# Seven products of quarters for the first MLP product of a two-layer trunk

## The chip, the cores and the metric

The kernel runs as one program on one core of a Trainium2 chip. The metric is the device time of one execution in microseconds. The kernel before takes 1731.39 us, the median of three runs (1730.09, 1731.39, 1732.92).

## The reference, cut to what matters

A trunk of two layers works on 16 learned and 512 given tokens of 1024 features, all in float32. Each layer is a sequence mixer and an MLP, each followed by a LayerNorm of the scaled input plus the result. The change touches the MLP alone:

```python
D_MODEL = 1024; D_FF = 4 * D_MODEL; DEPTH = 2

def sq_relu_mlp(h, w1, w2):
    return jnp.square(jax.nn.relu(h @ w1)) @ w2

# in each of the two layers, after the mixer:
h = layer_norm(DN_ALPHA * h + mix, ln1_w[i], ln1_b[i])
h = layer_norm(DN_ALPHA * h + sq_relu_mlp(h, mlp_w1[i], mlp_w2[i]), ln2_w[i], ln2_b[i])
```

Layer 0 has 528 tokens in its MLP. In layer 1 the 16 learned tokens are no longer needed there, so it has 512.

## The kernel before, in words

Everything is kept feature-major: 128 features on the partitions, tokens along the row. A float32 operand is kept as a pair, a rounded high part and the rest as a low part. One product of a 128 x 128 weight tile with a row of tokens is then three matmuls: high by high (line L173), high weight by low row (L174), low weight by high row (L175). A weight tile of 128 outputs by 1024 inputs is loaded by SyncE's queue (SP, L157, buffers `wr`, of which there are two) and split 512 columns at a time: ScalarE (ACT) rounds it into `wh` (L152), VectorE (DVE) subtracts into `wl` (L153). There are six buffers of each.

The 4096 hidden features of an MLP are taken in four groups of eight tiles. For each group, `mlp` first makes the eight tiles of `h @ w1`, eight steps of 128 inputs each. Each tile's sum in PSUM goes through ReLU (ACT, L381), a square in full precision (GpSimd, POOL, L383), a rounded square (ACT, L389) and the low part of it (DVE, L390). Then the eight output tiles take the product of this group with w2, again eight steps each, and DVE adds each sum from PSUM to a residual kept in SBUF (L363; in the first group L367 and L368, from the input of the MLP).

In layer 0 the 528 tokens are two halves of 272 and 256 columns. In layer 1 the two halves of 256 fit in one matmul of 512 columns; only the first three w1 tiles and the last three w2 tiles keep the halves apart, so that the norm before can still be under way and the norm after can begin with one half.

The order of the instructions on each engine is fixed when the program is built. The code is written as generators that are interleaved, and a scheduler then gives each engine its list. Each engine takes its list in order and waits at an instruction whose inputs or buffers are not ready. PSUM has eight banks, three for these sums (`pmm`) and five others (`pmx`).

Of the kernel before, what the change touches and what calls it, by code (L numbers as in the profile page):

```python
# [18 lines left out]
P = 128  # L19
# [38 lines left out]
def trunk(ctx: ExitStack, tc: tile.TileContext, a, out):  # L58
# [11 lines left out]
    NBUF = {"s": 40, "m": 20, "n": 40, "row": 3}  # L70
# [56 lines left out]
    # ---------------------------------------------------------------- constants  # L127
# [22 lines left out]
    # ---------------------------------------------------------------- weights  # L150
# [26 lines left out]
    def product(o, blks, xs, m=P, k0=0, k1=None, every=8):  # L177
        """o[m, n] += sum over k0 <= k < k1 of blks[k]^T xs[k]"""
        per = 512 // P if m == P else 8
        n = len(xs)  # L180
        for k in range(k0, k1 or n):
            hi, lo = blks[k // per]
            c = (k % per) * m
            mm3(o, (hi[:, c:c + m], lo[:, c:c + m]), xs[k], k == 0, k == n - 1)
            if k % every == every - 1 and k < n - 1:
                tick()

    def phase(tiles, rhs, evac, ns, head=0, tail=0, ready=None):
        """tiles: list of (srcs, key[, m]); rhs[half][k] = (hi, lo) APs, rhs[2] both halves where they fit a
        bank. In the first and the last tiles the halves are apart, so that what precedes and follows can  # L190
        work on one half at a time."""
        def both(blks, key):
            o = pm(512)
            product(o, blks, rhs[2], every=4)
            for hf in range(2):
                evac(key, hf, o[:, hf * 256:hf * 256 + 256])
            tick()

        def run(hf, blks, key, m=P):
            o = pm(ns[hf], part=m)  # L200
            product(o, blks, rhs[hf], m=m)
            evac(key, hf, o)
            tick()
        n = len(tiles)
        for i0, i1 in [(0, head)] + [(i, i + 1) for i in range(head, n - tail)] + [(n - tail, n)]:
            held = []
            for srcs, *key in tiles[i0:i1]:
                held.append(([b for s in srcs for b in (s if isinstance(s, list) else wload(s))], *key))
# [50 lines left out]
    def layernorm(r, ns, hf, go, apply, together=False):  # L259
        """statistics of the tokens of a half as its sums r come, then apply(off, bn, pt, mean, rstd, i)"""  # L260
# [49 lines left out]
    def norm_after(r, ns, wcol, bcol):  # L310
        """tasks for both halves, each from when its sums have been emitted"""
# [35 lines left out]
    def residual(hx, offs, ns, early=()):  # L347
        """evac into r = alpha * h + product"""
# [24 lines left out]
    def mlp(l, hx, ns, ready, r, evac0):  # L373
        w1, w2 = a["mw1"], a["mw2"]
        for c in range(4):
            u = [[None] * 8 for _ in hx]

            def evac_u(f, hf, o):
                n = ns[hf]
                t = tl("m", n)  # L380
                S.activation(t, o, AF.Relu)  # L381
                q = tl("m", n)
                G.tensor_tensor(q, t, t, op=MUL)  # L383
                if hf == 0:
                    pair = tl("s", L, F32R), tl("s", L, F32R)
                    for dst, x in zip(u, parts(pair, ((0, n), (n, ns[1]), (0, 512)))):
                        dst[f] = x
                hi, lo = u[hf][f]
                S.activation(hi, t, AF.Square)  # L389
                V.tensor_tensor(lo, q, hi.bitcast(F32), op=SUB)  # L390

            phase([([w1[l, c * 8 + f]], f) for f in range(8)], hx, evac_u, ns,
                  head=3 if c == 0 else 0, ready=ready if c == 0 else None)
            phase([([w2[l, c, m]], m) for m in range(KT)], u,
                  lambda m, hf, o: evac0(m, hf, o, last=c == 3), ns, tail=3 if c == 3 else 0)

    # ---------------------------------------------------------------- shared pieces
# [15 lines left out]
    def conv_job(src, wc, bcol, done):  # L413
        """projection through conv and silu, feature-major [128, L]"""
# [30 lines left out]
    def gate_job(src, width, task):  # L445
        """small projection, then a task on its sums"""
# [10 lines left out]
    def gate_task(fm, width):  # L457
        """token-major [128, 5, width] with unused rows zero"""
# [9 lines left out]
    def decay(dt_in, bias, alog, nh):  # L468
        """g = -exp(A_log) softplus(x + bias), sums over chunks and their exponentials"""
# [17 lines left out]
    # ================================================================ layer 0 mixer  # L487
# [15 lines left out]
    # scratch in DRAM for the diagonal blocks of 32: a pitch of 129 rows makes the 68 blocks equidistant  # L503
# [26 lines left out]
    def gdn_keys(hd):  # L530
# [3 lines left out]
        # decays between the tokens of a chunk  # L534
# [16 lines left out]
        # similarities of the keys; the squared norms are on their diagonal  # L551
# [32 lines left out]
    def gdn_base():  # L584
        """diagonal blocks of 32, one to a partition: forward substitution"""
# [341 lines left out]
    hn, _, ready = norm_after(r, ns0, PP_LN, PP_LN + 8)  # L927
# [4 lines left out]
    mlp(0, h, ns0, ready, r, ev)  # L932
    h = hn

    # ================================================================ layer 1 mixer
# [27 lines left out]
    def hb(ap):  # L963
        """[128, heads] over the 64 features of a head"""
# [188 lines left out]
    hn, _, ready = norm_after(r, ns1, PP_LN + 32, PP_LN + 40)  # L1153
    # the first products begin with the groups that are ready
# [20 lines left out]
    def finish(hf):  # L1175
# [16 lines left out]
        def last(blocks):  # L1192
            """both blocks at once, over the engines; what needs the mean alone comes first"""
# [23 lines left out]
    mlp(1, h, ns1, ready, r, ev)  # L1217
# [101 lines left out]
```

## Time and profile before

| | |
|---|---|
| median of the runs | 1731.39 us |
| span of the profiled execution, which is also its time from the first instruction to the last | 1727.4 us |
| TensorE (PE) busy | 1690.1 us, 98% |
| DVE, ACT, POOL busy | 1015.5, 680.0, 324.1 us |
| mean granted TensorE clock | 0.995 |
| DMA | 157.99 MB, 91 GB/s |

An engine's idle time costs nothing unless TensorE waits for it. A row of a group of instructions has the source line, the engine, the operation, the names of the tile written and of those read, their shapes, the count, then the busy time in us and the mean of one in ns, and last the idle time before them and what ended it. PEld is TensorE's loading of weights, which runs beside its matmuls.

### The profile page before, as it was taken

Reading aid. Unit: us, or ns where it says so; the run is one execution under the profiler, and the core shown is the slowest. Engines: PE = TensorE matmul, PEld = TensorE weight load, DVE = VectorE, ACT = ScalarE, POOL = GpSimd, SP = SyncE. Lnnn points to the kernel's source line nnn. Section 1 sums busy time; section 2 is a strip of 40 time slices with the busy share of each in tenths; the row PEclk is TensorE's granted clock in tenths of the full one; section 3 lists DMA queues with packets and bytes.
Section 4 is the critical chain, followed back from the end, with each engine's and each line's share of the span. In section 5 each row is a group of like instructions: output and inputs, shape, how many; then the busy total and the mean of one; then the engine's idle time right before and its main releaser. Section 6 shows DMA issues by size and latency. Waiting matters only on the chain.

```text
span 1727.4 us, 29456 instructions
## 1 busy us (share of the span) xinstructions
PE 1690.1 (98%) x11644; PEld 1537.0 (89%) x11644; DVE 1015.5 (59%) x2116; ACT 680.0 (39%) x1455; POOL 324.1 (19%) x380
## 2 busy tenths in 40 slices
PE   9999999999999999999999999999999999999997
PEld 8899998899999999999999878888788888888886
DVE  6896667676436443343348767868753744444345
ACT  4432345554225333242425634554432533333331
POOL 1311211010004111010202245242400411101012
PEclk9999999999999999999999999999999999999999
DMA  7224211112222222222221443333222222222221
GB/s 252 69 86 121 77 63 62 38 63 85 98 66 82 92 92 87 98 87 89 96 72 61 131 133 88 99 110 111 80 79 98 73 86 98 98 98 89 94 98 61
DMA packets 80325, 157.99 MB, mean 91 GB/s; under 512 B 12668, under 2 KB 45820, under 8 KB 79932
## 3 DMA queue, kind: packets, MB, share of 16 engines
q1 hardware_dynamic: 80044, 155.86, 28.2%
q8 instruction: 91, 1.49, 0.4%
q14 instruction: 46, 0.38, 0.1%
q10 hardware_dynamic: 144, 0.26, 0.0%
HBM read 149.95 MB, written 6.15 MB: 90 GB/s over the span
## 4 chain that ended last, share of the span: by engine, by line
PE 84%; DVE 6%; DMA 3%; POOL 3%; ACT 2%; issue 2%; SPq 0%; POOLq 0%; DVEq 0%; ACTq 0%
PE pmm L173 24%; PE pmm L175 24%; PE pmm L174 24%; DMA row<-rd 2%; DVE s L407 2%; DVE wl L153 2%; POOL row L985 1%; PE pmx L271 1%; POOL hl L341 1%; DMA wr<-in_w 1%; PE pmx L331 1%; PE pmx L1049 1%; PE pmx L1045 1%; POOL n L147 1%; PE pmx L753 1%
## 5 line engine op out<-in xcount | busy, mean ns | idle before, releaser
L173 PE MATMUL pmm<-hh,wh 128*128 128x272 f32 (+4 forms) x2104 | 652.3, 311 | 2.3 <-ACT wh L152 0.9
L174 PE MATMUL pmm<-hl,wh 128*128 128x272 f32 (+4 forms) x2104 | 638.5, 304 | 2.7 <-POOL hl L341 2.1
L175 PE MATMUL pmm<-hh,wl 128*128 128x272 f32 (+4 forms) x2104 | 640.3, 304 | 0.1
L153 DVE TENSOR_TENSOR wl<-wr,wh 128x512 fp32r<-128x512 f32 (+1 forms) x498 | 376.2, 759 | 319.8 <-ACT wh L152 313.5
L152 ACT CAST wh<-wr 128x512 fp32r<-128x512 f32 (+1 forms) x498 | 306.6, 619 | 628.3 <-PE pmm L174 605.1
L173 PEld LDWEIGHTS pmm<-hh,wh 128*128 128x128 f32 (+2 forms) x2104 | 393.5, 187 | 25.0 <-issue 4.4
L174 PEld LDWEIGHTS pmm<-hl,wh 128*128 128x128 f32 (+2 forms) x2104 | 393.6, 187 | 24.4 <-POOL hl L341 4.6
L175 PEld LDWEIGHTS pmm<-hh,wl 128*128 128x128 f32 (+2 forms) x2104 | 393.5, 187 | 17.0 <-DVE wl L153 0.3
L173 PE MATMUL pmm<-s,wh 128*128 128x256 f32 (+2 forms) x1192 | 377.9, 317 | 0.0
L175 PE MATMUL pmm<-s,wl 128*128 128x256 f32 (+2 forms) x1192 | 377.2, 317 | 0.0
L174 PE MATMUL pmm<-s,wh 128*128 128x256 f32 (+2 forms) x1192 | 376.4, 316 | 0.0
L174 PEld LDWEIGHTS pmm<-s,wh 128*128 128x128 f32 x1192 | 224.3, 188 | 15.5 <-DVE s L1124 0.3
L173 PEld LDWEIGHTS pmm<-s,wh 128*128 128x128 f32 x1192 | 224.4, 188 | 15.1
L175 PEld LDWEIGHTS pmm<-s,wl 128*128 128x128 f32 x1192 | 224.1, 188 | 15.0
L383 POOL TENSOR_TENSOR m<-m 128x256 f32<-128x256 f32 (+1 forms) x128 | 92.1, 729 | 536.0 <-ACT m L381 532.7
L147 POOL TENSOR_TENSOR n<-n,neg 128x1 f32<-128x1 f32 (+2 forms) x58 | 37.9, 657 | 462.7 <-DVE n L146 436.5
L390 DVE TENSOR_TENSOR s<-m,s 128x256 fp32r<-128x256 f32 (+1 forms) x128 | 64.3, 521 | 95.2 <-POOL m L383 93.2
L407 DVE SCALAR_TENSOR_TENSOR s<-s,pp,s 128x528 f32<-128x528 f32 x120 | 96.5, 804 | 25.8 <-ACT s L405 24.1
L363 DVE TENSOR_TENSOR m<-m,pmm 128x256 f32<-128x256 f32 (+1 forms) x108 | 43.7, 423 | 107.4 <-PE pmm L175 107.2
L381 ACT ACTIVATE m<-pmm 128x256 f32<-128x256 f32 (+1 forms) x128 | 48.7, 380 | 60.4 <-PE pmm L175 60.4
L985 POOL TENSOR_TENSOR row<-row,m 128x1024 f32<-128x1024 f32 x16 | 32.8, 2052 | 122.3 <-DMA row<-rd 78.3
L389 ACT ACTIVATE s<-m 128x256 fp32r<-128x256 f32 (+1 forms) x128 | 54.0, 422 | 3.9
(275 smaller groups left out, 1501.1 us busy)
## 6 DMA issues: line engine op xcount, KB each, us to landing
wr<-in_mw SPq DMA_DIRECT2D x128, 512.0 KB, 3.3
wr<-in_w SPq DMA_DIRECT2D x88, 512.0 KB, 3.3
wr<-in_wo SPq DMA_DIRECT2D x29, 512.0 KB, 3.5
row<-rd SPq DMA_DIRECT2D x16, 512.0 KB, 6.0
s<-rd SPq DMA_DIRECT2D x32, 128.0 KB, 6.1
out<-row SPq DMA_DIRECT2D x7, 256.0 KB, 2.0
wr<-in_wo SPq DMA_DIRECT2D x6, 256.0 KB, 3.0
dt<-row SPq DMA_DIRECT2D x3, 365.5 KB, 5.9
```

The lines of the kernel that those rows point to most:

```text
L147: G.tensor_tensor(dst, t, neg5[0:part, 0:n], op=POW)
L152: S.copy(dst_hi, src)
L153: V.tensor_tensor(dst_lo, src, dst_hi.bitcast(F32), op=SUB)
L173: T.matmul(o, w[0], x[0], start=first, stop=False)
L174: T.matmul(o, w[0], x[1], start=False, stop=False)
L175: T.matmul(o, w[1], x[0], start=False, stop=last)
L381: S.activation(t, o, AF.Relu)
L383: G.tensor_tensor(q, t, t, op=MUL)
L389: S.activation(hi, t, AF.Square)
L390: V.tensor_tensor(lo, q, hi.bitcast(F32), op=SUB)
L407: V.scalar_tensor_tensor(acc, cin[:, k:k + L], w[k], acc, op0=MUL, op1=ADD)
L985: G.tensor_tensor(g3(rw, 8), g3(rw, 8), bc(gc[:, c * 32 + 8 * g:c * 32 + 8 * g + 8], P), op=SUB)
```

## The change

The 4096 hidden features are now taken in eight groups of four tiles. The first two groups are computed as before, the second of them tile by tile in turn with two tiles of the first group's product with w2. In the six others two w1 tiles are taken together (`sevens`). They are seen as a 2 x 2 matrix of quarters (two tiles by two halves of the 1024 inputs), and the rows as a 2 x 2 matrix of quarters (two halves of the inputs by two halves of the tokens, 264 or 256 columns). Seven products of quarters, each four steps of three matmuls, take the place of eight, with sums and differences of weight quarters (s1 to s4) and of row quarters (`combos`, once per MLP). After each such pair of tiles come four tiles of the group before with w2, each of four steps. The w2 tiles are loaded in pieces of 256 KB.

```diff
-    NBUF = {"s": 40, "m": 20, "n": 40, "row": 3}
+    NBUF = {"s": 40, "m": 26, "n": 40, "row": 4}
...
+    def combos(pairs, nh, get):
+        q = slice(0, nh), slice(nh, 2 * nh)
+        def part(k, c, lo):
+            return pairs[k][lo][:, q[c]].bitcast(F32)
...
+        for k in range(4):
+            d1, d3, e = tl("m", nh), tl("m", nh), tl("m", nh)
+            G.tensor_tensor(d1, part(k, 1, 0), part(k, 0, 0), op=SUB)
+            V.tensor_tensor(e, part(k, 1, 1), part(k, 0, 1), op=SUB)
+            V.tensor_tensor(d1, d1, e, op=ADD)
+            get(0, k, d1)
+            yield
...
+    def sevens(srcs, keys, B, nh, evac):
+        raw1, raw2 = fetch(srcs[0]), fetch(srcs[1])
+        a11, a12, a21, a22 = [x[:, i:i + 512] for x in (raw1, raw2) for i in (0, 512)]
+        s12, s34 = tl("row", 1024), tl("row", 1024)
+        s1, s2, s3, s4 = [x[:, i:i + 512] for x in (s12, s34) for i in (0, 512)]
+        V.tensor_tensor(s1, a21, a22, op=ADD)
+        V.tensor_tensor(s3, a11, a21, op=SUB)
+        G.tensor_tensor(s2, s1, a11, op=SUB)
+        G.tensor_tensor(s4, a12, s2, op=SUB)
...
+        bank = [pm(nh)] + [px(nh) for _ in range(3)]
...
+        w11 = pair(a11, False)
+        prod(bank[0], w11, 0, True, False)
+        p1 = tl("m", nh)
+        S.copy(p1, bank[0])
+        prod(bank[1], pair(s2, True), 5, True, True)
+        V.tensor_tensor(p1, p1, bank[1], op=ADD)
+        tick()
+        prod(bank[2], pair(s3, True), 6, True, False)
+        u3 = tl("m", nh)
+        V.tensor_tensor(u3, p1, bank[2], op=ADD)
+        prod(bank[3], pair(s1, True), 4, True, False)
+        V.tensor_tensor(u3, u3, bank[3], op=ADD)
+        evac(keys[1], 1, u3)
+        tick()
+        prod(bank[0], pair(a12, False), 1, False, True)
+        evac(keys[0], 0, bank[0])
+        prod(bank[2], pair(a22, False), 3, False, True)
+        c21 = tl("m", nh)
+        V.tensor_tensor(c21, p1, bank[2], op=ADD)
+        evac(keys[1], 0, c21)
+        tick()
+        prod(bank[3], pair(s4, True), 2, False, True)
+        V.tensor_tensor(p1, p1, bank[3], op=ADD)
+        evac(keys[0], 1, p1)
+        tick()
...
+        u, ev = group()
+        phase([([w1[l, f]], f) for f in range(GF)], hx, ev, ns, head=3, ready=ready)
+        spawn(combos(pairs, nh, get))
...
+            if c == 1:
+                for f in range(GF):
+                    phase([([w1[l, GF + f]], f)], hx, evn, ns)
+                    second(0, u, 2 * f, 2 * f + 2)
...
+                for i in range(2):
+                    sevens([w1[l, c * GF + i], w1[l, c * GF + i + 2]], (i, i + 2), B, nh,
+                           lambda f, hf, o: evn(f, hf, o, nh))
+                    second(c - 1, u, 4 * i, 4 * i + 4)
...
-    nc = bacc.Bacc("TRN2", target_bir_lowering=False, num_devices=1)
+    nc = bacc.Bacc("TRN2", target_bir_lowering=False, num_devices=1, dynamic_dma_scratch_size=1024)
```

What the scheduler makes of it is shown at three places in layer 0's MLP, in steady state. Line numbers from here on are those of the changed kernel: L433 is the matmul in `prod`, L413 to L416 are s1, s3, s2, s4, L441, L445, L447, L454 the sums from PSUM, L490 the square on POOL, L497 its low part on DVE. Numbers behind names tell buffers apart.

On POOL, before, a stretch of w1 tiles:

```order
L383 TENSOR_TENSOR m_8006<-m_8004 128x272
L383 TENSOR_TENSOR m_8039<-m_8037 128x256
L383 TENSOR_TENSOR m_8080<-m_8078 128x272
L383 TENSOR_TENSOR m_8113<-m_8111 128x256
L383 TENSOR_TENSOR m_8154<-m_8152 128x272
```

and now, the end of one block and the rest of the next:

```order
L490 TENSOR_TENSOR m_9135<-m_9133 128x264
L415 TENSOR_TENSOR row_9352<-row_9352,wr_9348 128x512
L416 TENSOR_TENSOR row_9353<-wr_9348,row_9352 128x512
L490 TENSOR_TENSOR m_9159<-m_9157 128x264
L490 TENSOR_TENSOR m_9185<-m_9183 128x264
L490 TENSOR_TENSOR m_9208<-m_9206 128x264
```

The two sums for the next block (wr_9348) stand between the first and the second square of the present one.

On DVE, before, at the same w1 tiles:

```order
L390 TENSOR_TENSOR s_8009<-m_8006,s_8008 128x272
L153 TENSOR_TENSOR wl_8194<-wr_8191,wh_8193 128x512
L153 TENSOR_TENSOR wl_8198<-wr_8191,wh_8197 128x512
L390 TENSOR_TENSOR s_8009<-m_8039,s_8008 128x256
L390 TENSOR_TENSOR s_8083<-m_8080,s_8082 128x272
```

and now, in one block (pmx_9060 to pmx_9062 are its banks, row_9054 holds its s4, wr_9348 and wr_9350 are the next block's weights):

```order
L153 TENSOR_TENSOR wl_9283<-wr_9280,wh_9282 128x512
L153 TENSOR_TENSOR wl_9317<-wr_9314,wh_9316 128x512
L441 TENSOR_TENSOR m_9079<-m_9079,pmx_9060 128x264
L445 TENSOR_TENSOR m_9114<-m_9079,pmx_9061 128x264
L447 TENSOR_TENSOR m_9114<-m_9114,pmx_9062 128x264
L413 TENSOR_TENSOR row_9352<-wr_9350 128x512
L414 TENSOR_TENSOR row_9353<-wr_9348,wr_9350 128x512
L497 TENSOR_TENSOR s_9138<-m_9135,s_9137 128x264
L153 TENSOR_TENSOR wl_9363<-wr_9348,wh_9362 128x512
L497 TENSOR_TENSOR s_9162<-m_9159,s_9161 128x264
L454 TENSOR_TENSOR m_9181<-m_9079,pmx_9061 128x264
L153 TENSOR_TENSOR s_9190<-row_9054,s_9189 128x512
```

The last row, the low part of the present block's s4, comes behind the next block's s1 and s3, the split of its first quarter, and the low part that reads m_9159, POOL's second square. In layer 1 one more split of the next block stands before it.

On TensorE, now, at the last of the block's seven products (pmx_9062) and the first w2 tile (pmm_9218):

```order
L173 MATMUL pmm_9218<-s_8563,wh_9214 128x272
L174 MATMUL pmm_9218<-s_8564,wh_9214 128x272
L175 MATMUL pmm_9218<-s_8563,wl_9215 128x272
L173 MATMUL pmm_9218<-s_8862,wh_9214 128x272
L433 MATMUL pmx_9062<-hh_6677,s_9189 128x264
L433 MATMUL pmx_9062<-hl_6678,s_9189 128x264
L174 MATMUL pmm_9218<-s_8863,wh_9214 128x272
L175 MATMUL pmm_9218<-s_8862,wl_9215 128x272
L173 MATMUL pmm_9218<-s_8539,wh_9214 128x272
L174 MATMUL pmm_9218<-s_8540,wh_9214 128x272
L175 MATMUL pmm_9218<-s_8539,wl_9215 128x272
L433 MATMUL pmx_9062<-hh_6677,s_9190 128x264
```

Eleven matmuls stand between the end of the sixth product and the first that reads s4's low part (s_9190); nine of them are the w2 tile's.

More of the change, by code (lines that the diff above doesn't have):

```diff
@@ L207, in phase @@
             for srcs, *key in tiles[i0:i1]:
-                held.append(([b for s in srcs for b in (s if isinstance(s, list) else wload(s))], *key))
+                held.append(([b for s in srcs for b in (s if isinstance(s, list) else s() if callable(s) else wload(s))], *key))
                 if len(rhs) > 2 and head <= i0 < n - tail:
@@ L371, in residual, with diff @@
         return r, evac
-    def mlp(l, hx, ns, ready, r, evac0):
-        w1, w2 = a["mw1"], a["mw2"]
[L375 to L379, printed above, removed]
+    def combos(pairs, nh, get):
+        q = slice(0, nh), slice(nh, 2 * nh)
+        def part(k, c, lo):
+            return pairs[k][lo][:, q[c]].bitcast(F32)
+        def diff(out, a, b, engine):
+            engine.tensor_tensor(out, a, b, op=SUB)
+        for k in range(4):
[5 more added lines that the diff above has]
+            yield
+            G.tensor_tensor(d3, part(k + 4, 1, 0), part(k, 1, 0), op=SUB)
+            V.tensor_tensor(e, part(k + 4, 1, 1), part(k, 1, 1), op=SUB)
+            V.tensor_tensor(d3, d3, e, op=ADD)
+            get(2, k, d3)
+            yield
+            d2, d4 = tl("m", nh), tl("m", nh)
+            G.tensor_tensor(d2, part(k + 4, 1, 0), d1, op=SUB)
+            V.tensor_tensor(d2, d2, part(k + 4, 1, 1), op=ADD)
+            get(1, k, d2)
+            yield
+            G.tensor_tensor(d4, part(k + 4, 0, 0), d2, op=SUB)
+            V.tensor_tensor(d4, d4, part(k + 4, 0, 1), op=ADD)
+            get(3, k, d4)
+            yield
@@ new lines, in sevens, with pair, prod @@
+    def sevens(srcs, keys, B, nh, evac):
[7 more added lines that the diff above has]
+        G.tensor_tensor(s4, a12, s2, op=SUB)
+        def pair(x, big):
+            if big:
+                hi, lo = tl("s", 512, F32R), tl("s", 512, F32R)
+            else:
+                hi = sb.tile([P, 512], F32R, tag="wh", bufs=6, name=nm("wh"))
+                lo = sb.tile([P, 512], F32R, tag="wl", bufs=6, name=nm("wl"))
+            split(hi, lo, x)
+            return hi, lo
+        bank = [pm(nh)] + [px(nh) for _ in range(3)]
+        def prod(o, w, b, first, last):
+            for k in range(4):
+                c = slice(k * P, (k + 1) * P)
+                for i, (x, y) in enumerate(((0, 0), (0, 1), (1, 0))):
+                    T.matmul(o, w[x][:, c], B[b][k][y], start=first and k == i == 0, stop=last and k == 3 and i == 2,
+                             skip_group_check=True)
+        w11 = pair(a11, False)
[23 more added lines that the diff above has]
+        tick()
@@ new lines, in mlp, with get, half, group @@
+    def mlp(l, hx, ns, ready, r, evac0, pairs):
+        w1, w2 = a["mw1"], a["mw2"]
+        nh = (ns[0] + ns[1]) // 2
+        NG, GF = 8, 4
+        tt = [[None] * 4 for _ in range(4)]
+        def get(j, k, x):
+            hl = tl("s", 2 * nh, F32R)
+            split(hl[:, 0:nh], hl[:, nh:2 * nh], x)
+            tt[j][k] = hl[:, 0:nh], hl[:, nh:2 * nh]
+        def half(k, i):
+            return tuple(x[:, i * nh:(i + 1) * nh] for x in pairs[k])
+        def group():
+            u = [[None] * GF for _ in hx]
+            us = [None] * GF
+            def evac_u(f, hf, o, n=None):
+                if n is None:
+                    n, off = ns[hf], hf * ns[0]
+                else:
+                    off = hf * n
@@ L926, in trunk @@
     r, ev = residual(h, (0, 0), ns0, early=range(5, KT))
-    hn, _, ready = norm_after(r, ns0, PP_LN, PP_LN + 8)
+    hn, hp, ready = norm_after(r, ns0, PP_LN, PP_LN + 8)
     phase([([a["wo0"][m, :, 0:1024], a["wo0"][m, :, 1024:2048]], m) for m in range(KT)], y, ev, ns0, tail=2)
@@ L931, in trunk @@
     hn, hx, ready1 = norm_after(r, ns0, PP_LN + 16, PP_LN + 24)
-    mlp(0, h, ns0, ready, r, ev)
+    mlp(0, h, ns0, ready, r, ev, hp)
     h = hn
@@ L1152, in trunk @@
     r, ev = residual(h, (16, 0), ns1, early=range(5, KT))
-    hn, _, ready = norm_after(r, ns1, PP_LN + 32, PP_LN + 40)
+    hn, hp, ready = norm_after(r, ns1, PP_LN + 32, PP_LN + 40)
     until(lambda: yw[2][11] is not None)
@@ L1216, in trunk @@
     spawn(finish(1))
-    mlp(1, h, ns1, ready, r, ev)
+    mlp(1, h, ns1, ready, r, ev, hp)
     drain()
```

26 lines of the change are left out of this document (18 added, 8 removed).

## The prediction

> **What bounds the kernel now.** First the busy shares and the chain of work that ended last, on the profile's page:
>
> ```profile
> PE 1690.1 (98%) x11644; PEld 1537.0 (89%) x11644; DVE 1015.5 (59%) x2116; ACT 680.0 (39%) x1455; POOL 324.1 (19%) x380
> PE 84%; DVE 6%; DMA 3%; POOL 3%; ACT 2%; issue 2%; SPq 0%; POOLq 0%; DVEq 0%; ACTq 0%
> ```
>
> TensorE is busy 98% of the span and is 84% of the chain. The table by windows inside the two MLPs says at what rate:
>
> ```profile
> 600.00:700.00 100.00, 100.00 (x822) 100.00 (x821) 41.93 (x78) 33.52 (x67) 11.81 (x16) 1.00 0.28 90
> 1500.00:1690.00 190.00, 190.00 (x822) 154.06 (x822) 78.03 (x138) 65.10 (x133) 22.52 (x32) 1.00 0.28 95
> ```
>
> Columns: stretch, length, PE, weight loads, DVE, ACT, POOL, clock, DMA. In layer 0 one product (272 and 256 columns in turn, 264 in the mean) takes 100/822 = 0.1217 us; in layer 1 one of 512 columns takes 190/822 = 0.2311 us. TensorE never stops there, so fewer columns are worth exactly their time, as long as the other engines stay ahead. The changed layer 1 uses 256 columns, whose interval is in the timeline:
>
> ```profile
> 599.80 0.29 PE L173 MATMUL pmm<-s,wh 128*128 128x256 f32 x1
> ...
> 600.87 0.29 PE L173 MATMUL pmm<-s,wh 128*128 128x272 f32 x1
> ```
>
> Nine 256-column products lie between these starts: 1.07/9 = 0.1189 us. Each lasts 0.29 us, so a sum can be read 0.17 us after its last interval ends.
>
> **What it removes.** One block (two w1 tiles) has 84 products where there were 96 (layer 0), or 48 of 512 columns (layer 1). Layer 0: 12 x 0.1217 = 1.46 us. Layer 1: 48 x 0.2311 - 84 x 0.1189 = 11.09 - 9.99 = 1.10 us. Twelve blocks each: 17.5 + 13.2 = **30.7 us less** on TensorE. The w2 columns are only regrouped.
>
> **What it adds beside TensorE.** A block and the four w2 tiles after it form a period of 21.9 us of TensorE work in layer 0 (180 x 0.1217). The durations, from the groups of instructions kept apart by form:
>
> ```profile
> L153 DVE TENSOR_TENSOR wl<-wr,wh 128x512 fp32r<-128x512 f32 x66 | 45.7, 692 | 43.4 <-ACT wh L152 41.4
> L363 DVE TENSOR_TENSOR m<-m,pmm 128x272 f32<-128x272 f32 x19 | 8.3, 437 | 33.4 <-PE pmm L175 33.4
> L390 DVE TENSOR_TENSOR s<-m,s 128x272 fp32r<-128x272 f32 x16 | 7.1, 442 | 35.0 <-POOL m L383 32.9 <-POOL s L416 2.1
> L152 ACT CAST wh<-wr 128x512 fp32r<-128x512 f32 x104 | 64.5, 621 | 140.3 <-PE pmm L174 139.0 <-DMA wr<-in_mw 1.3
> L381 ACT ACTIVATE m<-pmm 128x272 f32<-128x272 f32 x27 | 10.7, 397 | 48.4 <-PE pmm L175 48.4
> L389 ACT ACTIVATE s<-m 128x272 fp32r<-128x272 f32 x27 | 11.7, 432 | 0.9
> L383 POOL TENSOR_TENSOR m<-m 128x272 f32<-128x272 f32 x32 | 20.4, 640 | 196.5 <-ACT m L381 194.6 <-issue 1.9
> L1203 POOL TENSOR_TENSOR row<-row,lnf 128x512 f32<-128x512 f32 x1 | 1.3, 1263 | 0.8 <-ACT row L1202 0.8
> L175 PEld LDWEIGHTS pmm<-s,wl 128*128 128x128 f32 x1192 | 224.1, 188 | 15.0
> wr<-in_mw SPq DMA_DIRECT2D x128, 512.0 KB, 3.3
> wr<-in_wo SPq DMA_DIRECT2D x6, 256.0 KB, 3.0
> ```
>
> DVE per period: 11 splits and 2 sums of 512 columns at 0.69, 5 sums and 8 residual additions at 0.44, 4 low parts at 0.44: 16.5 us. ACT: 11 casts at 0.62, a copy at 0.40, 4 times 0.83: 10.5 us. POOL: 2 sums at 1.26 and 4 squares at 0.64: 5.1 us. All fit in 21.9 us, so no engine is bound by its total; the order decides.
>
> **The wait that I expect.** The scheduler makes the sums s1 to s4 of the next block inside the present one. On DVE the low part of s4 of the present block stands behind s1 and s3 of the next, two low parts and c21; one of these low parts needs a square that stands on POOL behind s2 and s4 of the next block. TensorE needs that low part for its third s4 product. Walk for layer 0, zero at the block's start: six products of 12 end at 8.76; with the 11 products put between, the low part is due at 10.10. The fourth product can be read at 6.0; L447 ends at 6.5. s1 needs the second w1 tile, whose transfer is issued behind the last w2 tile's split (its buffer waits for the first product, 1.63; then 0.62 and 0.69: 3.0), and lands 3.3 later at 6.3: in time. s1 ends at 7.2.
>
> From here it matters whether DVE and POOL hold each other up. Three pairs in the timeline (start, length):
>
> ```profile
> 560.59 0.69 DVE L153 TENSOR_TENSOR wl<-wr,wh 128x512 fp32r<-128x512 f32 x1 [0.73 <-ACT wh L152]
> 560.98 0.77 POOL L383 TENSOR_TENSOR m<-m 128x256 f32<-128x256 f32 x1 [2.55 <-ACT m L381]
> 968.76 1.90 POOL L985 TENSOR_TENSOR row<-row,m 128x1024 f32<-128x1024 f32 x1 [1.05 <-DMA row<-rd]
> 969.35 1.86 DVE L153 TENSOR_TENSOR wl<-wr,wh 128x512 fp32r<-128x512 f32 x1 [3.56 <-ACT wh L152]
> 1018.81 1.90 POOL L985 TENSOR_TENSOR row<-row,m 128x1024 f32<-128x1024 f32 x1 [5.99 <-DMA row<-rd]
> 1019.12 0.69 DVE L1006 TENSOR_TENSOR s<-pmx,m 128x512 f32<-128x512 f32 x1
> ```
>
> In the first, POOL's square ends at 561.75, 0.47 us after DVE's split (561.28). In the second, the split takes 1.86 instead of 0.69 and ends at 971.21, 0.55 us after POOL's sum (970.66). So of two operations on SBUF alone the later one waits for the other's end, and is then short by about 0.15 us, its start-up. In the third, DVE reads one input from PSUM and is not held (0.69 under POOL's 1.90). I take it that the two engines alternate where both have work ready. [...]
>
> With alternation: square of u3 to 7.67, s3 8.22, s2 (1.26 - 0.15) 9.33, low part of u3 (0.44 - 0.15) 9.62, s4 10.73, split of the next w11 11.28, the awaited square 11.75, its low part 12.22, c21 12.62, low part of s4 13.28, and with 0.04 and a weight load of 0.19 TensorE goes on at 13.5: **3.4 us of stall** per block. In layer 1 the low part is due at 72 x 0.1189 + 8 x 0.2311 + 2 x 0.1189 = 10.65; on DVE the split of the next a12 stands before it too, and POOL's next square slips in: 14.35, stall **3.7 us**. Without exclusion the same walk gives 12.55 and 12.95, so 2.45 and 2.3 us. The last block of a layer has no next one, so no sums are in its way; I estimate 1 us there. Eleven blocks each: 11 x (3.4 + 3.7) + 2 = **80 us**; without exclusion 11 x 4.75 + 1 = 53. I take 80, since the pairs fit exclusion; 53 is the lower bound. The upper one is the clock's, below. After the stall DVE has slack under the w2 tiles (10.6 us of TensorE against some 8), so the period does not grow further.
>
> **The combinations of h.** They fall into the second group: TensorE has 384 x 0.1217 = 46.7 us there, 192 x 0.2311 = 44.4 in layer 1. From the first combination to the last w2 evacuation DVE has 21 operations of 512 columns, 49 small ones and 32 residual ones: 14.5 + 21.6 + 14.0 = 50.1 us; POOL 24 x 0.64 + 2 x 1.26 = 17.9, of which 7.0 can lie under residual operations that read PSUM and 26 x 0.15 under start-ups. That is 57.1 against the 48.3 us until DVE would be late: +8.8, in layer 1 +9.8, **19 together**. Bounds: POOL wholly beside, +5; wholly between, +40.
>
> **The end of each MLP.** The last three w2 tiles of the second half cover the norm of the first, and now have 12 instead of 24 products each. Before, from the chain and the windows:
>
> ```profile
> 898.22 0.92 PE pmx L271 x8
> 908.60 2.45 PE pmx L331 x13
> 900.00:905.00 5.00, 5.00 (x45) 5.00 (x44) 4.65 (x14) 2.55 (x5) 1.07 (x2) 1.00 0.35 108
> ```
>
> DVE is full under that cover (4.65 of 5); 36 products less take 4.3 us of it. I take 4 us at layer 0, where the next layer waits for the norm, and 1 us at the end: **5**, bounds 0 and 8.6. Edits at nothing: the 256 KB transfers of w2 (3.0 us to land, issued 3 us or more ahead under a w2 tile's 2.9 us; without that cover some 1 us a block), the casts on ACT, more buffers, the smaller scratch.
>
> **Sum.** -30.7 + 80 + 19 + 5 = +73: span 1727.4 + 73 = 1800.8. The profiled execution is 4.0 us below the median of the runs, 1731.4; so **1805**.
>
> **Rivals.** (a) DVE and POOL run side by side: -30.7 + 53 + 5 + 3 = +30, **1762**. For it: the sums are other operations than the two pairs; against it: both pairs fit exclusion to a few hundredths. (b) Other side: s4's low part comes in time because POOL does its two sums well under the 1.26 of its row, or under TensorE; then -30.7 + 5 + 3 = -23, **1709**. It decides once the mean stall is below 0.3 us with the combinations as forecast, below 1.0 with their lower bound. Against it: s1 and s3, the two sums and the square are all ahead of that low part in the fixed orders, and 6.5 to 10.1 is too short for 1.26 + 1.26 + 0.64 alone with s1. (c) The stalls let the clock fall. It fell here 4.2 us after the last product (1716.7):
>
> ```profile
> 1716.00:1717.00 1.00, 0.44 (x2) 0.20 (x2) 0.58 (x2) 0.00 (x0) 0.00 (x0) 1.00 0.63 250
> 1720.00:1721.00 1.00, 0.00 (x0) 0.00 (x0) 1.00 (x2) 0.68 (x1) 0.29 (x1) 0.96 0.00 0
> 1721.00:1722.00 1.00, 0.00 (x0) 0.00 (x0) 0.90 (x2) 0.05 (x1) 0.88 (x1) 0.50 0.28 111
> ```
>
> Of the stalls the part in one piece is 2.8 us, in layer 1 3.2. If it trips in layer 1 and half speed lasts as long as the 4.2 us seen, each block loses 2.1 more: 1805 + 23 = **1828**. [...]
>
> **Chances.** Forecast 0.58, (a) 0.22, (b) 0.10, (c) 0.10. Faster by over 0.2% 0.09, within 0.2% 0.02, slower 0.89; 0.2% (3.5 us) is about what a measurement of this kernel can tell from no change. The range runs from below (a) to above (c): 1750 to 1840; the forecast's own is 1780 to 1830.
>
> **What would show it.** In the profile after, TensorE waits for the split on DVE (L153) at the sevens' matmul line L433, some 22 times at 2.5 to 3.5 us; blocks of 25 us where 23.4 were; DVE's L153 mean well above 0.69. Clock 1.00 throughout refutes (c); L153 and POOL's sums at their quiet durations support (a). The forecast is wrong if TensorE is still gapless in 650 to 900 us, or if the stall sits elsewhere, as at a transfer.

## The result: slower by 6.4%

The changed kernel takes 1841.4 us (median of 4 runs, 1840.0 to 1843.7), before 1730.7 us (1729.1 to 1732.9): ratio 1.0641, 95% interval 1.0626 to 1.0656, 110.7 us more. The forecast was 1805 in 1750 to 1840: the direction was right, the size 36 us short, and the time lies 1.4 us above the range.

The profile's page of the changed kernel, busy shares, chain by engine and the row of the granted clock:

```profile
PE 1711.4 (93%) x11896; PEld 1564.8 (85%) x11896; DVE 1272.9 (69%) x2564; ACT 732.1 (40%) x1583; POOL 444.4 (24%) x460
PEclk9999999999999999999998999999999999899898
PE 60%; DVE 12%; POOL 9%; issue 8%; DMA 7%; ACT 3%; SPq 0%; POOLq 0%; DVEq 0%; ACTq 0%
```

TensorE was busy 98% of the span and is now 93%, though it has fewer columns to work through. Its busy time is even longer (1711.4 against 1690.1 us), which fewer products cannot explain: some of them ran slower. The view of waits, TensorE's own (us in total, times, longest):

```profile
PE pmx L433 <- DVE s L153: 72.7, 24, 4.3
PE pmm L173 <- DVE m L367: 12.8, 5, 5.5
```

The first row is the forecast's wait, for the low part of s4 (split on DVE, L153) at the sevens' products (L433); the second is in the second group, where the combinations of h are made. The table by windows over the groups with sevens in layer 0 and in layer 1 (columns as in the prediction: length, PE, weight loads, DVE, ACT, POOL, clock, DMA):

```profile
615.00:929.00 314.00, 275.08 (x2088) 271.38 (x2087) 210.91 (x349) 111.25 (x234) 76.07 (x72) 0.94 0.24 79
1485.00:1793.00 308.00, 267.54 (x1547) 232.80 (x1546) 208.62 (x368) 114.78 (x241) 80.12 (x75) 0.92 0.25 82
```

Before, TensorE was busy in all of such a stretch, at clock 1.00. Now it is idle 38.9 and 40.5 us there, and the clock is 0.94 and 0.92: (1 - 0.94) x 314 + (1 - 0.92) x 308 = 19 + 25 = 43 us of full-speed work lost at most. At most, because this mean also counts half speed while TensorE has nothing to do: by the trace's records of the clock, half speed was granted for 37.5 us of the first stretch and 47.8 of the second, and TensorE was busy in 36.5 and 38.9 of them. Half of that busy time, 18.2 + 19.4, is about **38 us** that the forecast's sum did not have. One block of layer 0 in the timeline, TensorE, DVE and POOL in this order (start, length, engine, line):

```profile
680.48 0.28 PE L175 MATMUL pmm<-s,wl 128*128 128x272 f32 x1
684.05 0.79 PE L433 MATMUL pmx<-hh,s 128*128 128x264 f32 x2 [3.29 <-DVE s L153]
...
677.82 1.12 DVE L414 TENSOR_TENSOR row<-wr,wr 128x512 f32<-128x512 f32 x1
678.87 1.54 DVE L497 TENSOR_TENSOR s<-m,s 128x264 fp32r<-128x264 f32 x1
680.33 1.78 DVE L153 TENSOR_TENSOR wl<-wr,wh 128x512 fp32r<-128x512 f32 x1
682.62 0.43 DVE L497 TENSOR_TENSOR s<-m,s 128x264 fp32r<-128x264 f32 x1 [0.52 <-POOL m L490]
683.32 0.69 DVE L153 TENSOR_TENSOR s<-row,s 128x512 fp32r<-128x512 f32 x1
...
677.39 1.01 POOL L490 TENSOR_TENSOR m<-m 128x264 f32<-128x264 f32 x1 [16.20 <-ACT m L488]
678.36 1.76 POOL L415 TENSOR_TENSOR row<-row,wr 128x512 f32<-128x512 f32 x1
680.19 1.37 POOL L416 TENSOR_TENSOR row<-wr,row 128x512 f32<-128x512 f32 x1
681.52 1.07 POOL L490 TENSOR_TENSOR m<-m 128x264 f32<-128x264 f32 x1
```

DVE and POOL take turns: the low part at 678.87 lasts 1.54 where it lasts 0.43 alone at 682.62, and ends 0.29 behind POOL's sum (678.36 to 680.12); the split at 680.33 lasts 1.78 in the place of 0.69 and ends 0.55 behind POOL's second sum (680.19 to 681.56). Only then come the awaited square and the low part of s4 (683.32), and TensorE has stood idle 3.29 us. What follows on TensorE is in the table by windows of 1 us (the ninth column is the clock):

```profile
683.00:684.00 1.00, 0.00 (x0) 0.00 (x0) 1.00 (x4) 0.57 (x2) 0.07 (x1) 1.00 0.00 0
684.00:685.00 1.00, 0.94 (x4) 0.95 (x5) 1.00 (x2) 1.00 (x3) 1.00 (x1) 0.55 0.00 0
685.00:686.00 1.00, 1.00 (x7) 1.00 (x6) 0.98 (x2) 0.20 (x1) 0.09 (x1) 0.50 0.28 66
686.00:687.00 1.00, 1.00 (x6) 1.00 (x6) 0.36 (x1) 0.00 (x0) 0.00 (x0) 0.50 0.61 195
687.00:688.00 1.00, 1.00 (x9) 1.00 (x8) 0.75 (x3) 0.90 (x3) 0.40 (x1) 0.74 0.09 27
688.00:689.00 1.00, 1.00 (x11) 1.00 (x10) 1.00 (x2) 0.56 (x3) 0.23 (x1) 1.00 0.00 0
```

Work starts again at 684.05, and the clock is at half speed from there for about 3.4 us: 6 or 7 products in a microsecond where the last row, at 1.00, has 11. This happens behind each of the 11 long waits of layer 0. Layer 1 has one block where the clock stayed up, next to one where it did not, with equal work, which gives the price within one execution (wait, work, wait, work):

```profile
1658.72:1662.03 3.31, 0.01 (x1) 0.01 (x1) 2.81 (x6) 1.23 (x4) 1.99 (x3) 1.00 0.00 0
1662.03:1683.60 21.57, 21.57 (x132) 18.81 (x132) 14.01 (x26) 8.26 (x18) 4.26 (x5) 1.00 0.30 98
1683.60:1687.10 3.50, 0.00 (x0) 0.00 (x0) 3.00 (x6) 1.22 (x4) 2.18 (x3) 1.00 0.00 0
1687.10:1710.25 23.15, 23.14 (x132) 20.16 (x132) 14.63 (x26) 8.38 (x18) 4.44 (x5) 0.93 0.29 92
```

The same 132 products take 21.57 us at clock 1.00 and 23.15 at 0.93: 1.58 us for one fall of the clock. Elsewhere in layer 1 half speed lasts up to 6.8 us at a time, and a block loses up to 2.5 us (24.06 us of work, from 1740.01 to 1764.07, in the place of 21.57).

Against the forecast's sum: -30.7 of products, 72.7 of waits for s4, 38 of clock, 12.8 for the combinations and some 2 of clock behind their wait in layer 0 make 95 of the 114.5 us between the two profiled spans (1727.4 and 1841.9). The first activation of the first MLP comes 4.2 us later than before (532.9 against 528.7, timeline). The way from the end of the first MLP to the first activation of the second is 6.6 us longer (451.0 against 444.4, from the start of the last sum into the residual). The clock may have a part in both: ahead of the first MLP it is at half speed for 10.2 us in this execution and never in the one before, and between the MLPs for 13.7 us against 10.2; how much of the two it makes was not traced. About 9 us are left. Some 4 of them, by an estimate, are 24 x 0.17 us, by which the last product ahead of each of the 24 waits outlasts its interval (0.29 us against 0.12 in the timeline) while the views count it as busy. The rest stays open.

### The profile page after: what moved, and what is told of

The parts are those of the page before. It is cut to its first block, busy times and chain, and to the rows that moved or that the text cites. A ratio compares the mean times of both kernels' runs of the same rounds, so it can differ in the third digit from the quotient of the medians.

```text
span 1841.9 us, 30663 instructions
## 1 busy us (share of the span) xinstructions
PE 1711.4 (93%) x11896; PEld 1564.8 (85%) x11896; DVE 1272.9 (69%) x2564; ACT 732.1 (40%) x1583; POOL 444.4 (24%) x460
## 4 chain that ended last, share of the span: by engine, by line
PE 60%; DVE 12%; POOL 9%; issue 8%; DMA 7%; ACT 3%; SPq 0%; POOLq 0%; DVEq 0%; ACTq 0%
PE pmm L173 15%; PE pmm L175 15%; PE pmm L174 15%; DMA wr<-in_mw 4%; PE pmx L433 4%; DVE wl L153 3%; DMA row<-rd 3%; POOL m L490 2%; POOL row L415 2%; POOL row L416 2%; DVE s L153 1%; DVE s L536 1%; PE pmm L433 1%; ACT wh L152 1%; POOL row L1114 1%
## 5 line engine op out<-in xcount | busy, mean ns | idle before, releaser
L153 DVE TENSOR_TENSOR wl<-wr,wh 128x512 fp32r<-128x512 f32 (+1 forms) x474 | 382.3, 810 | 158.9 <-ACT wh L152 150.6
L173 PE MATMUL pmm<-hh,wh 128*128 128x256 f32 (+5 forms) x1528 | 470.4, 308 | 5.5 <-ACT s L529 1.7
L174 PE MATMUL pmm<-hl,wh 128*128 128x256 f32 (+5 forms) x1528 | 457.1, 299 | 2.7 <-POOL hl L341 1.9
L175 PE MATMUL pmm<-hh,wl 128*128 128x256 f32 (+5 forms) x1528 | 457.6, 300 | 0.0
L173 PEld LDWEIGHTS pmm<-hh,wh 128*128 128x128 f32 (+2 forms) x1528 | 287.2, 188 | 20.5 <-issue 4.2
L174 PEld LDWEIGHTS pmm<-hl,wh 128*128 128x128 f32 (+2 forms) x1528 | 287.0, 188 | 15.5 <-POOL hl L341 4.0
L175 PEld LDWEIGHTS pmm<-hh,wl 128*128 128x128 f32 (+2 forms) x1528 | 286.8, 188 | 8.6 <-DVE wl L153 0.2
L490 POOL TENSOR_TENSOR m<-m 128x256 f32<-128x256 f32 (+2 forms) x128 | 109.6, 858 | 506.1 <-ACT m L488 504.0
L363 DVE TENSOR_TENSOR m<-m,pmm 128x256 f32<-128x256 f32 (+1 forms) x236 | 94.9, 421 | 128.1 <-PE pmm L175 128.1
L433 PE MATMUL pmx<-hh,s 128*128 128x264 f32 (+1 forms) x192 | 60.8, 393 | 72.8 <-DVE s L153 72.7
L433 PEld LDWEIGHTS pmx<-hh,s 128*128 128x128 f32 x192 | 44.0, 266 | 85.9 <-DVE s L153 80.5
L497 DVE TENSOR_TENSOR s<-m,s 128x256 fp32r<-128x256 f32 (+2 forms) x128 | 85.7, 672 | 35.3 <-POOL m L490 34.6
```

The costliest lines, as they stand in the source:

```text
L153: V.tensor_tensor(dst_lo, src, dst_hi.bitcast(F32), op=SUB)
L173: T.matmul(o, w[0], x[0], start=first, stop=False)
L174: T.matmul(o, w[0], x[1], start=False, stop=False)
L175: T.matmul(o, w[1], x[0], start=False, stop=last)
L363: V.tensor_tensor(t, t, o, op=ADD)
L433: T.matmul(o, w[x][:, c], B[b][k][y], start=first and k == i == 0, stop=last and k == 3 and i == 2, skip_group_check=True)
```

## Experiments

Three theories were to be told apart. **A**: the order, TensorE waits because the low part of s4 stands late on DVE. **B**: exclusion, DVE is late because POOL's sums and squares hold it up. **C**: the clock, which falls behind the waits, is a cost of its own. Besides, the terms for the combinations, the ends of the MLPs and the regrouping were measured alone. All times are medians. Before, measured beside them, had 1729.6 us (first four), 1730.2 (next four) and 1730.5 (last four).

### Order alone: the splits early

```diff
-        w11 = pair(a11, False)
+        w11, w2_, w3_, w1_ = pair(a11, False), pair(s2, True), pair(s3, True), pair(s1, True)
+        w12, w22, w4_ = pair(a12, False), pair(a22, False), pair(s4, True)
...
-        prod(bank[3], pair(s4, True), 2, False, True)
+        prod(bank[3], w4_, 2, False, True)
```

> All seven weight operands of a block are split at its start, before its first product, where the changed kernel splits each just ahead of its own product; nothing else is changed, the number of instructions is the same. In the fixed order of DVE the low part of s4 then stands a block of work earlier, so TensorE should not wait for it. Theory (the wait for s4's low part, 38.9 us in layer 0 and 33.8 in layer 1, and the clock that falls behind it, about 19 and 25 us, make the loss): 1841.4 - 73 - 43 = 1725 us where no other wait takes the place, and up to 1770 where DVE and POOL, which hold each other up and have 16.5 + 5.1 us of work in a period of 21.9, are the next limit with 1 to 2 us per block. The row of TensorE's line L433 waiting for the split on DVE is gone. Rival (DVE and POOL are full whatever the order, or the wait is for the weights' transfer): 1820 to 1845, with the same idle time under another name.

Measured: 1774.5 us, ratio 1.0256 (1.0234 to 1.0279), 67 us less than the changed kernel, just above the expected 1725 to 1770. TensorE's waits:

```profile
PE pmm L173 <- DVE m L363: 31.8, 30, 2.3
PE pmm L173 <- DVE m L367: 12.4, 5, 5.0
```

The wait at L433 is gone, and with it most of the falls of the clock (mean 0.984, after 0.966). In its place TensorE waits 30 times for evacuations (L363), about 1.6 us in a block of layer 0: DVE and POOL still hold each other up (splits at L153 last up to 1.8 us where 0.69 is quiet), and DVE reaches the evacuations late. So A explains the place of the wait, and not all of the loss.

### The clock: products in the pause

```diff
-        prod(bank[2], pair(a22, False), 3, False, True)
+        w22 = pair(a22, False)
+        prod(bank[2], w22, 3, False, True)
+        spare = px(nh)
+        for _ in range(2):
+            prod(spare, w22, 3, True, True)
```

> 24 more products per block, read by nobody, stand between the a22 and the s4 products: 24 x 0.12 = 2.9 us of the 3.5 us in which TensorE otherwise stands idle. The wait for s4's low part stays where it is. Theory (the clock falls because TensorE stands idle for 3.3 us or more in one piece, and about 43 us of the result are half-speed products): the granted clock is 1.00 through both MLPs and the time is 1841.4 - 43 = 1798 us, 1795 to 1810. Rival (the lower clock comes with the load and not with the idle piece, or costs nothing because DVE sets the period): 1835 us or more, since products are added and none removed.

Measured: 1864.2 us (1852.7 to 1868.0), ratio 1.0760 (1.0721 to 1.0800): 23 us more than the changed kernel where 43 less were expected. The expectation forgot that the order changes: in the changed kernel nine products of the second product already lie ahead of the third s4 product, and here they all went behind it. The low part was due at 72 + 24 + 2 = 98 products (11.9 us) in the place of 83 (10.1), not 2.9 us later. So the wait shrank by 1.3 us a block only ((72.7 - 42.4) / 24), for 2.9 us of added products. It did shorten the pauses, and what the clock does then can be read. Waits, and windows around one pause:

```profile
PE pmx L433 <- DVE s L153: 42.4, 22, 3.3
...
706.78:708.63 1.85, 0.00 (x1) 0.01 (x1) 1.44 (x4) 0.63 (x2) 0.51 (x2) 1.00 0.00 0
708.63:709.63 1.00, 1.00 (x8) 1.00 (x9) 1.00 (x2) 1.00 (x3) 1.00 (x1) 1.00 0.00 0
709.63:710.63 1.00, 1.00 (x10) 1.00 (x10) 1.00 (x3) 0.66 (x2) 0.03 (x1) 1.00 0.05 16
```

After 1.85 us of idle time the clock stays at 1.00. In layer 0 it fell behind 3 of 11 pauses (one of 2.97 us, and ones of 2.09 and 1.73) where it fell behind all 11 in the changed kernel; the mean clock is 0.984. The sum is 24 blocks x 2.9 us = 70 added, 30 less of waiting and, by the mean clock (1 - 0.966) x 1841.9 - (1 - 0.984) x 1850.9, 33 less of half speed (27 of it while TensorE was busy): +7 to +13 us, against +9 between the two profiled spans. (The runs of this kernel spread more than others; its profiled execution is near their lower end.) That agrees with theory C, though the time alone, which was to decide, went the other way. What shows C is the pair of blocks above, with equal work inside one execution.

### Regrouping alone, and the ends of the MLPs

```diff
-        spawn(combos(pairs, nh, get))
...
-                    sevens([w1[l, c * GF + i], w1[l, c * GF + i + 2]], (i, i + 2), B, nh,
-                           lambda f, hf, o: evn(f, hf, o, nh))
+                    phase([([w1[l, c * GF + 2 * i + j]], 2 * i + j) for j in range(2)], hx, evn, ns)
```

and the same with the last six tiles in halves:

```diff
-        second(NG - 1, u, 0, KT, tail=3)
+        second(NG - 1, u, 0, KT, tail=6)
```

> The regrouping alone: eight groups of four tiles of the first product, two of them in turn with four tiles of the second, the buffers of the changed kernel, but no seven products and no combinations (eight products, as before). Theory: the loss is in the sevens and the combinations, so this is before's time plus what the smaller cover at the ends of the MLPs costs: 1731 to 1742 us. Rival (the regrouping itself, its 256 KB transfers or the changed scratch cost time): 1750 us or more.

> The regrouping alone (eight products, no combinations), with the last six w2 tiles of each MLP in halves where there were three. It measures the term for the ends of the MLPs: theory, the 8 us by which the regrouping alone is slower than before are the smaller cover under the norm (forecast 5 us), so this is 1730 to 1733 us. Rival (the 8 us are the regrouping's transfers or its changed scratch): 1737 us as without it.

Measured: 1737.8 us, ratio 1.0047 (1.0034 to 1.0061), and 1732.1 us, ratio 1.0011 (1.0001 to 1.0020). Regrouping costs 8 us, and 6 of them go with the longer tail. Both are as expected. The profiled executions do not show it (spans of 1731.4 and 1732.2 us), so the size rests on the medians, and where the 6 us lie was not seen.

### The combinations left out

```diff
-        spawn(combos(pairs, nh, get))
...
-                     [half(k, 1) for k in range(4, 8)], tt[3], tt[0], tt[1], tt[2]]
+                     [half(k, 1) for k in range(4, 8)]]
+                B += [[half(k, 1) for k in range(4)], B[0], B[1], B[2]]
```

> The sevens with plain quarters of h in the place of the four combinations; it leaves out the combinations of h (112 operations with their casts in each layer), so that the output is not the reference's, and all else is as in the changed kernel. Theory: the second group loses its 7.3 and 5.5 us of idle time and the lower clock behind it, 9 and 8 us: 1841.4 - 17 = 1824 us; the waits for s4's low part stay, 38.9 and 33.8 us. Forecast of the prediction for this term: 19 us. Rival (the combinations are hidden, and the wait moves on): 1838 us or more.

Measured: 1831.7 us, ratio 1.0587 (1.0558 to 1.0616): the combinations cost 10 us by the medians (15 by the profiled spans), not 17 or 19. The waits for s4 are as they were:

```profile
PE pmx L433 <- DVE s L153: 74.5, 24, 4.3
```

### What POOL does, piece by piece

A block has two kinds of work on POOL: the sums s2 and s4, and the squares of the activations. The edits are these two lines each:

```diff
-        G.tensor_tensor(s2, s1, a11, op=SUB)
-        G.tensor_tensor(s4, a12, s2, op=SUB)
+        V.tensor_tensor(s2, s1, a11, op=SUB)
+        V.tensor_tensor(s4, a12, s2, op=SUB)
```

```diff
-                G.tensor_tensor(q, t, t, op=MUL)
+                S.activation(q, t, AF.Square)
```

With the early splits:

> The early splits, and in addition the sums s2 and s4 on DVE in the place of POOL. POOL's two sums took 1.69 and 1.38 us between DVE's operations, on DVE they take 0.69 each. Theory (with the early splits TensorE waits 31.8 us for evacuations at L363 because DVE and POOL hold each other up): 3.1 us of POOL become 1.4 us of DVE per block, so the 1.0 to 1.7 us of wait per block go nearly to nothing: 1774.5 - 25 to 32 = 1742 to 1750 us. Rival (DVE's own work is the limit, and more of it makes it worse): 1775 us or more.

> The early splits, and the squares that POOL computes for the low parts of the activations on ACT instead; the sums s2 and s4 stay on POOL. Four squares of 0.64 to 1.17 us per block leave POOL, and ACT gets four of 0.43. Theory: the squares are the smaller part of what POOL holds DVE up with (4 x 0.64 against 3.1 us), so the waits at L363 fall by about half: 1774.5 - 10 to 20 = 1755 to 1765 us. Rival (the splits on DVE alone set the period): 1774 us.

> The early splits, sums on DVE and squares on ACT together, so that POOL has nothing to do in a block, and the last six w2 tiles of each MLP in halves where there were three, which gives back the cover that the norm of the first half had before. Theory: no wait per block is left (DVE 16.5 + 1.4 us in 21.9), the combinations still cost about 17 us, the ends nothing: 1730.7 - 30.7 + 17 + 6 = 1723 us, 1715 to 1735. Rival (something else of the sevens costs as much as they save, such as the longer chain of banks): 1745 us or more.

With the changed kernel's late splits:

> The changed kernel's late splits, with the sums s2 and s4 on DVE and the squares on ACT: nothing of a block is on POOL. In DVE's order s1, s3, s2, s4, two low parts, c21 and one split stand ahead of the low part of s4. Theory: without the exclusion that low part is ready 11.85 us after the block's start and due at 10.45, so 1.4 us of wait per block stay, 31 us in all, too short to bring the clock down: 1841.4 - (73 - 31) - 43 = 1756 us, 1745 to 1768, and clock 1.00 behind the waits. Rival (the order alone makes the wait, whoever does the sums): wait of 3 us or more per block, clock 0.50 behind it, 1820 us or more.

> The changed kernel with late splits, the sums s2 and s4 on POOL as there, and only the squares on ACT. The low part of s4 is due at 10.95 us (90 products, seven more of the second product are put ahead of it) and by the walk ready at 13.4: a wait of 2.4 us per block in the place of 3.3, the clock half of the time down, and the combinations without their 13 us of idle time: 1841.4 - 20 - 21 - 17 = 1783 us, 1765 to 1805. Rival (the square is what the low part waits for, and POOL's sums hurt little): waits under 1 us and 1735 us.

> The changed kernel with late splits, the squares on POOL as there, and only the sums s2 and s4 on DVE. The low part of s4 is due at 11.07 us (91 products) and by the walk ready at 12.75: a wait of 1.7 us per block, too short to bring the clock down in most blocks; the combinations keep their 13 us of idle time: 1841.4 - 37 - 38 = 1766 us, 1750 to 1785. Rival (DVE gets longer by the sums and the wait stays): 1820 us or more.

| splits | sums s2, s4 | squares | us | ratio to before (95%) |
|---|---|---|---|---|
| late (the change) | POOL | POOL | 1841.4 | 1.0641 (1.0626 to 1.0656) |
| late | POOL | ACT | 1792.7 | 1.0348 (1.0324 to 1.0372) |
| late | DVE | POOL | 1763.9 | 1.0183 (1.0166 to 1.0200) |
| late | DVE | ACT | 1732.3 | 1.0011 (0.9996 to 1.0026) |
| early | POOL | POOL | 1774.5 | 1.0256 (1.0234 to 1.0279) |
| early | DVE | POOL | 1741.7 | 1.0056 (1.0040 to 1.0072) |
| early | POOL | ACT | 1732.6 | 1.0018 (1.0007 to 1.0028) |
| early, last six tiles in halves | DVE | ACT | 1708.3 | 0.9865 (0.9849 to 0.9880) |

TensorE's wait at L433 with the late splits: squares on ACT, then sums on DVE, then both.

```profile
PE pmx L433 <- DVE s L153: 50.0, 22, 3.7
```

```profile
PE pmx L433 <- DVE s L153: 22.3, 23, 2.2
```

```profile
PE pmx L433 <- DVE s L153: 7.9, 11, 2.0
```

Emptying POOL takes 109 us off the changed kernel although DVE gets two more operations per block and its late splits stay: work on POOL is the larger cause. Two things go with it. DVE's operations get shorter: its busy time falls from 1272.9 to 1219.5 us although 48 sums of 0.68 us have come to it, so the rest takes 86 us less; that is theory B. And DVE no longer waits for POOL's squares, for which it waited 34.6 us in the changed kernel (24.2 us for ACT's squares now). How much of TensorE's wait goes to each is not shown by these runs.

Of the six, 1792.7 and 1763.9 us came as expected and 1741.7 just below its range; 1732.6, 1732.3 and 1708.3 us lie 22, 13 and 7 us below theirs. The walks for the two single steps were good to some 10 us (1783 and 1766 expected). For both steps together 1756 was expected and 1732 came: that walk took the third s4 product to be due at 10.45 us, as measured after the change, while in this order 19 or 20 products lie between the a22 product and it where there were 11. It is due at 91 x 0.1217 = 11.1 us, and the low part is ready some 0.5 us after that. With early splits the squares cost more than was thought (42 us, where 10 to 20 were expected), the sums 33 (25 to 32).

The last row of the table beats the kernel before by 1.35%. Its page:

```profile
PE 1660.8 (98%) x11932; PEld 1530.7 (90%) x11932; DVE 1216.6 (71%) x2612; ACT 765.3 (45%) x1711; POOL 266.7 (16%) x284
```

TensorE has 29.3 us less to do than before, and is again busy 98%. No wait of 0.8 us or more is left in the sevens, and the wait for the combinations (L367 above, 12.8 us) is down to one of 1.6 us, where the expectation still took 17 us for them. Early splits and an empty POOL with the old end of three tiles were not run, so of the 24 us between this row and 1732.3 the longer tail has a part, 6 us where it was measured alone.

### Exclusion alone: POOL work that nobody waits for

```diff
         V.tensor_tensor(s4, a12, s2, op=SUB)
+        G.tensor_tensor(idle[:, 0:512], a21, a11, op=SUB)
+        G.tensor_tensor(idle[:, 512:1024], a21, a12, op=SUB)
```

added to the 1708.3 us version.

> The version with early splits and nothing of a block on POOL (1708.3 us), with two differences of weight quarters per block computed on POOL whose results nobody reads. No instruction waits for them. Theory (DVE and POOL exclude each other while both work on SBUF): DVE's splits, 0.69 us when quiet, become longer wherever a POOL operation of 1.3 to 1.7 us stands in their way, 2.5 to 3 us of DVE's time are lost per block, the low parts and evacuations come late again and the time rises by 10 to 25 us, to 1718 to 1733. Rival (the loss of the kernels with work on POOL came from waiting for POOL's results): 1708 us, within 3, and DVE's durations unchanged.

Measured: 1757.9 us, ratio 1.0149 (1.0131 to 1.0167): 50 us more for 48 operations whose results nobody reads, twice the upper end of what was expected. DVE and POOL in one block (s3 and s2 are now L416 and L417 on DVE), then TensorE's waits:

```profile
664.72 1.79 DVE L416 TENSOR_TENSOR row<-wr,wr 128x512 f32<-128x512 f32 x1
666.43 1.77 DVE L417 TENSOR_TENSOR row<-row,wr 128x512 f32<-128x512 f32 x1
...
664.25 1.71 POOL L419 TENSOR_TENSOR idle<-wr,wr 128x512 f32<-128x512 f32 x1 [20.94 <-DMA wr<-in_mw]
665.93 1.73 POOL L420 TENSOR_TENSOR idle<-wr,wr 128x512 f32<-128x512 f32 x1
...
PE pmm L173 <- DVE m L363: 22.6, 19, 2.7
PE pmx L437 <- DVE m L450: 8.1, 9, 1.4
```

Without this work the two DVE operations last 0.68 us each. Here they last 1.79 and 1.77, each ending 0.54 to 0.55 us after the POOL operation in its way (665.96 and 667.66). That is 2.2 us of DVE per block, 24 x 2.2 = 53 us in all, and the span grew by 55 (1703.3 to 1758.1). The rival, that only waits for POOL's results cost time, is refuted: in the trace no instruction and no transfer waits for these two operations. The expectation was too low because it gave DVE's slack of the whole period as cover. The slack lies under the w2 tiles, where DVE waits for TensorE (67.1 us ahead of L363 in the 1708.3 us version, by the groups of instructions); in the block itself DVE's chain is what TensorE waits for. In sum the span grew by about what DVE lost: TensorE's idle time by 33 us (75.9 against 42.5), its busy time by 21 (1682.2 against 1660.8), part of it at half speed (mean clock 0.989 against 0.996).

## Why the prediction was wrong

**What held.** Fewer products: -30.7 us forecast, 29.3 less of TensorE's busy time in the version without waits. The wait for the low part of s4: 80 us forecast, 72.7 measured, at the line, the engine and the instruction named; 3.4 us per block in layer 0 forecast, 3.3 to 3.5 in 8 of its 11 long pauses; in layer 1, where 3.7 was forecast, most are 3.3 to 3.5, and one is 1.5. The walk was right to a few tenths: in the block shown the low part starts 13.0 us after the block's first product (670.31 in the timeline), 12.6 by the walk. Exclusion was taken from two pairs of rows and extended to other operations; the alternation shows in the block above and alone in the last experiment, the 0.55 us behind POOL's end too. The ends of the MLPs: 5 us forecast, 6 by the medians.

**The step that failed** is rival (c), the clock, which the sum left out. It said that the part of a stall in one piece is 2.8 us, in layer 1 3.2, that the clock might trip in layer 1 at 2.1 us a block, and gave that a chance of 0.10. Measured: the pieces are 3.0 to 4.3 us but for one, the clock fell in both layers, at 1.5 to 2.5 us a block, about **38 us** in all against the 23 of the rival and the 0 of the forecast. With 38 the forecast would have been 1843, 2 us from the result; that it comes so near is luck, since the waits for s4 and the combinations were forecast too dear and other pieces were not in the sum. Three things were wrong in the step. The piece was taken half a microsecond shorter than the stall in both layers; in the trace nearly all of a stall is one piece (3.29 idle of the 3.45 by which the next product is late in the block shown). The price of 2.1 us was half of 4.2 us, but those 4.2 us are the length of a pause, not of a stretch at half speed; such stretches lasted 3.4 us, or 6.8. And the 4.2 us seen at the end of the trace of before was read as if it were the least that trips the clock. No row showed that a piece of 3.2 us leaves it up, and the same trace has half speed from 1010.94 us on, between the MLPs, behind a pause of 2.04 us (1007.98 to 1010.02). In the runs the clock fell behind 25 of the 50 pauses of 1.7 to 2.7 us (below).

**Rival (a)**, no exclusion, was priced with 53 us of waits. No run shows what POOL's work would cost without the exclusion. With nothing on POOL the waits came to 10 us (7.9 for the split and 2.3 for a cast). Part of the difference is that the two sums take 0.68 us each on DVE where the walk had 1.26 on POOL, and part the scheduler: its order had eight more products ahead of the due one, 1 us per block. A walk along one order gives a price for that order only.

**Rival (b)** fell with the main wait. In (a) and (b) the last two terms, 5 and 3 us, stand without a derivation; measured were 10 us for the combinations and 6 for the ends. **The combinations**, 19 us, were about twice too dear: 10 us by the medians, and their wait almost vanishes when the squares leave POOL, which points to POOL's load and not DVE's total.

"All fit in 21.9 us, so no engine is bound by its total; the order decides" was half of the truth: with the order mended alone 45 us of the loss remained (1774.5 against 1729.6), with POOL emptied alone 2 us.

## What to carry to other kernels

Before moving element-wise work to POOL, look whether DVE's operations of that stretch have both inputs in SBUF. Such operations lasted 1.79 and 1.77 us beside POOL's here, 0.68 without, while one that read PSUM kept its 0.69 under 1.90 of POOL; and of the 53 us that DVE lost on the chain that TensorE waits for, nearly all came through (55 in the span). A repeated wait on TensorE is to be priced with what the clock takes behind it, which here added about half of the wait again (38 us on 72.7); behind pauses of 0.8 to 1.7 us half speed came only 3 times in 113. And when an experiment or an edit passes through a scheduler, count again what lies ahead of the product that waits.

## What the chip showed that was not expected

The clock falls behind much shorter pauses than the 4.2 us at the end of the trace of before. The table has every pause of TensorE over 0.8 us that begins at full clock in the two MLPs (first activation to last sum into the residual), in all fourteen profiles, and how often half speed was granted from then to four microseconds after it:

| pause, us | number | followed by half speed |
|---|---|---|
| 0.8 to 1.7 | 113 | 3 |
| 1.7 to 2.7 | 50 | 25 |
| 2.7 to 3.2 | 9 | 6 |
| over 3.2 | 44 | 42 |

The records of the granted clock in the traces show what goes with it besides the length. In each of the fourteen, half speed begins and ends only at points of a fixed grid of 3.413 us (the last stretch of a trace ends with the record). Of the 76 times that it was granted in the two MLPs, 56 lasted one step of the grid, 19 two and one three. And what goes with a fall is how much of one step TensorE was idle. From 520 us on in the fourteen traces, half speed followed 24 of the 60 full-speed steps that were idle for 45 to 55%, 105 of the 106 above, and 2 of all those below. In the traces of before and of the changed kernel alone it followed 4 of 10, 23 of 24, and none of 668. The two pauses of the equal blocks above differ in just this. In the table by windows, the first two rows are the two steps of the grid that share the first pause, and the third is the step that has most of the second; the last is the step after it:

```profile
1656.91:1660.32 3.41, 1.81 (x8) 0.91 (x6) 2.91 (x3) 0.56 (x2) 2.99 (x3) 1.00 0.02 5
1660.32:1663.73 3.41, 1.71 (x12) 1.66 (x13) 3.41 (x7) 2.27 (x5) 1.15 (x1) 1.00 0.21 77
1684.21:1687.62 3.41, 0.52 (x4) 0.52 (x5) 2.91 (x6) 1.74 (x5) 1.99 (x2) 1.00 0.04 8
1687.62:1691.03 3.41, 3.41 (x13) 3.02 (x13) 2.49 (x6) 1.46 (x4) 0.61 (x1) 0.50 0.22 68
```

Idle for 47 and 50% of a step, the clock stayed up; idle for 85%, it fell. By this grid a pause alone under 1.7 us can't fill half of a step (3 falls in 113), one over 3.4 us fills half of some step wherever it lies (over 3.2 us, 42 falls in 44), and between them it depends on its place on the grid.

Layer 0's mixer, in which nothing was changed, ends up to 5 us earlier or later in these kernels (first long pauses of the first MLP between 539.9 and 545.1 us). Why was not looked into.
